# Retention decays carried by per-head rotary tables instead of decayed copies of queries and keys

## The chip, the cores and the metric

The kernel runs on one core of a Trainium2 chip. The metric is the device time of one execution in microseconds (us), as the median of three runs. Engine names are those of the profile: PE is TensorE (PEld its weight loads), DVE is VectorE, ACT is ScalarE, POOL is GpSimd, SP is the engine that issues most DMAs from one queue, in order.

## The reference

One step of a one-layer encoder on 1024 prompt frames and 8 streams of 16 new frames: 1152 tokens, nine tiles of 128 (tiles 0 to 7 are the prompt, tile 8 holds the streams). A projection feeds differential attention and retention, their outputs a second projection, and then a gated MLP with a convolution. The change concerns retention only:

```
qr = rotary(heads(qr), pos)
kr = rotary(heads(kr), pos) * R_K_DIM ** -0.5
def retention_chunk(state, q, k, v, log_gamma):          # per head, L tokens
    decay  = where(i >= j, gamma ** (i - j), 0)
    o      = ((q k^T) * decay) v + (q state) * gamma ** (i + 1)
    state  = gamma ** L * state + (k * gamma ** (L - 1 - j))^T v
```

with four heads and gamma of head h equal to 1 - 2^(-5-h).

## The kernel before

**Stages.** Start and first projections; attention over the prompt; attention of the streams against their caches (the "decode" stage, from about 462 us); retention (from about 560 to 645 us); output projection; MLP. In all of them PE takes projection work in small pieces ("dense units") between the pieces of the stage itself: `fill(ns)` puts in dense matmuls worth so many ns while any are left. The order of PE's instructions is that of the program; a scheduler orders those of the other engines and of SP's queue.

**Rotary.** `evac` takes a projected tile of 128 tokens and two heads out of PSUM. For `qr` and `kr` it multiplies by cosine and sine (three DVE operations, L242 to L245), adds on POOL (L246), and stores the result to the DRAM scratch `d_qr` or `d_kr`. The table of a tile comes by a load into `cs` (L238, two buffers), or, for the last `qr` unit, from `rope`, which is loaded whole in the decode stage (L810).

**Retention.** The loop goes over the tiles in the order 8, 0, 1, ..., 7. In step n, `rflip(t)` transposes the queries of tile t (L959, copied by ACT to `QT`) and its keys (L969, copied to `KT`), and makes decayed copies `Qd` (DVE, L965) and `Kd` (POOL, L975). `rout(t-1)` then does the previous tile: L994 is `AT` times values, L996 is `Qd` times state, L1000 is `Kd` times values for the state update. After it `load_t(t+1)` loads queries, keys and values of the tile after next (L952) into the tags `ldqr`, `ldkr`, `ldvr`, two buffers each: tile t+1 takes the buffers of tile t-1. Last in the step `rscore(t)` does L983, and DVE multiplies by the decay mask to make `AT` (L985).

So PE's order in one step is L959, L969 (tile t), L994/L996, L1000 (tile t-1), L983 (tile t), and then L959, L969 of tile t+1. The output of a tile is normalised and stored to `d_on` (L1041); `pro` reads it back (`on`, L910) and multiplies it by `sgr` (L912) on POOL for the next stage.

Of the kernel before, what the change touches and what calls it, by code (L numbers as in the profile page):

```python
# [32 lines left out]

C_ID, C_J, C_J16, C_SELD, C_SEL, C_HALF, C_SUM = 0, 128, 256, 384, 512, 768, 770
C_W = 802
R_DP, R_QP, R_KP, R_KE, R_KO, R_DS, R_QE, R_QO = 0, 512, 1024, 1028, 1032, 1036, 1548, 2060
R_P, R_W = 1036, 2572
TH, CW = NTOK // 2, NTOK // 4
ORD = (0, 4, 1, 5, 2, 6, 3, 7, 8)
GROUPS = (2, 2, 4, 3, 4, 3, 4)  # L40
# [8 lines left out]
def body(ctx: ExitStack, tc: tile.TileContext, i):  # L49
    nc = tc.nc  # L50
    V, S, G, T = nc.vector, nc.scalar, nc.gpsimd, nc.tensor
# [58 lines left out]
    aux = wst.enter_context(pool("stg", side="right"))  # L110
# [67 lines left out]
    units, pend, prog = [], [], {"cur": None, "bal": 0.0, "now": 0.0, "done": 0, "lim": 99, "rope": None}  # L178
# [51 lines left out]
    def evac(pfx, c, t, ps_, rope=None):  # L230
        d = dst_of(pfx, c)(t)
        sg = aux.tile([128, 256], F32, tag="sg", bufs=3, name="sg")
        if pfx in ("qr", "kr"):
            if rope is not None:
                cs = rope[:, t]
            else:
                cs = aux.tile([128, 2, 64], F32, tag="cs", bufs=2, name="cs")
                nc.sync.dma_start(cs, i["rope"][t * 128:(t + 1) * 128])  # L238
            tm = aux.tile([128, 2, 2, 64], F32, tag="rot", bufs=2, name="rot")
            pv = ps_.rearrange("p (h a d) -> p h a d", h=2, a=2)  # L240
            sb = cs[:, 1].unsqueeze(1).to_broadcast([128, 2, 64])
            V.tensor_tensor(out=sg.rearrange("p (a d) -> p a d", d=64), in0=ps_.rearrange("p (a d) -> p a d", d=64),  # L242
                            in1=cs[:, 0].unsqueeze(1).to_broadcast([128, 4, 64]), op=ALU.mult)
            V.scalar_tensor_tensor(out=tm[:, :, 0], in0=pv[:, :, 1], scalar=-1.0, in1=sb, op0=ALU.mult, op1=ALU.mult)
            V.tensor_tensor(out=tm[:, :, 1], in0=pv[:, :, 0], in1=sb, op=ALU.mult)  # L245
# [24 lines left out]
    with ExitStack() as st:  # L270
# [176 lines left out]
        for tok in "a0 w0 a1 w1 x5 a2 w2 a3 x6 x7 a4 x8 a5 a6 a7 w3".split():  # L447
            z_, n = tok[0], int(tok[1:])
# [48 lines left out]
        for n_, nm in enumerate(("lambda_q1", "lambda_k1", "lambda_q2", "lambda_k2")):  # L497
# [10 lines left out]
                               in1=ident_all[:, C_HALF:C_HALF + 1], op0=ALU.mult, op1=ALU.add)  # L508
# [26 lines left out]
    with ExitStack() as st:  # L535
# [158 lines left out]
        for n_ in range(8 * NH):  # L694
            h, qb = divmod(n_, 8)
# [18 lines left out]
    with ExitStack() as st:  # L714
        dp = st.enter_context(pool("dec"))
# [101 lines left out]
        for b in range(NB + 1):  # L817
            if b < NB:
# [3 lines left out]
                KT = dflip(b)  # L822
# [103 lines left out]
    with ExitStack() as st:  # L926
        rp = st.enter_context(pool("ret"))
# [9 lines left out]
        def c4(off):
            if off < R_P:
                return rc[:, off:off + 512].rearrange("p (h c) -> p h c", h=NH)
            c_ = rp.tile([128, NH, 128], F32, tag="Qd" if off == R_QO else "os", bufs=2, name="c4")  # L940
            nc.sync.dma_start(c_.rearrange("p h c -> p (h c)"), i["rpack"][:, off:off + 512])
            return c_
# [12 lines left out]
        def rflip(t):  # L955
            q, k, v = lds[t]
            pq = rt()
            for h in range(NH):
                T.transpose(pq[:, h], q[:, h], ident)  # L959
            QT = rp.tile([128, NH, 128], F32, tag="QT", bufs=2, name="QT")  # L960
            S.copy(QT, pq)
            qd = []
            for off in ((R_QP,) if t < 8 else (R_QE, R_QO)):
                x_ = rp.tile([128, NH, 128], F32, tag="KT" if qd else "Qd", bufs=2, name="Qd")
                V.tensor_tensor(out=x_, in0=pq, in1=c8[off] if t == 8 else c4(off), op=ALU.mult)  # L965
                qd.append(x_)
            pk = rt()
            for h in range(NH):
                T.transpose(pk[:, h], k[:, h], ident)  # L969
            KT = rp.tile([128, NH, 128], F32, tag="KT", bufs=2, name="KT")  # L970
            S.copy(KT, pk)
            kd = []
            for off in ((R_KP,) if t < 8 else (R_KE, R_KO)):
                x_ = rp.tile([128, NH, 128], F32, tag="QT" if kd else "Kd", bufs=2, name="Kd")
                G.tensor_tensor(out=x_, in0=k, in1=rc[:, off:off + 4].unsqueeze(2).to_broadcast([128, NH, 128]),  # L975
                                op=ALU.mult)
                kd.append(x_)
            return QT, KT, qd, kd
# [597 lines left out]
def _consts():  # L1576
# [3 lines left out]
    f = np.float32  # L1580
    n = np.arange(128)
# [22 lines left out]
    even = (n // 16) % 2 == 0  # L1604
    for h in range(NH):
        g = 1.0 - 2.0 ** (-5.0 - h)
        dec = np.where(ii >= jj, g ** np.maximum(ii - jj, 0), 0.0) * sc
        c = slice(h * 128, h * 128 + 128)
        rp[:, R_DP:][:, c] = dec
        rp[:, R_DS:][:, c] = np.where(ii // 16 == jj // 16, dec, 0.0)  # L1610
        rp[:, R_QP:][:, c] = g ** (n + 1.0)[None]
        rp[:, R_QE:][:, c] = (g ** (t16 + 1.0) * even)[None]
        rp[:, R_QO:][:, c] = (g ** (t16 + 1.0) * ~even)[None]
        rp[:, R_KP + h] = g ** (127.0 - n) * sc
        rp[:, R_KE + h] = g ** (15.0 - t16) * even * sc
        rp[:, R_KO + h] = g ** (15.0 - t16) * ~even * sc
# [38 lines left out]
```

## Time and profile before

| | |
|---|---|
| median of three runs | 1551.61 us (1546.86 to 1553.54) |
| the profiled execution | 1546.16 us, of which the span is 1544.3 us |
| PE busy | 1502.5 us, 97% of the span |
| DVE, ACT, POOL busy | 964.3, 601.4, 232.2 us |
| mean granted clock of PE | 0.990 |

The span runs from the first to the last instruction. An engine's busy share is a mean over all stages; PE's pieces overlap in the array, so a busy PE is not one at its peak. A row of the timeline gives start, duration, engine, line, operation, output and inputs, and in brackets the idle time ahead of it with what ended it.

### The profile page before, as it was taken

Reading aid. Unit: us, or ns where it says so; the run is one execution under the profiler, and the core shown is the slowest. Engines: PE = TensorE matmul, PEld = TensorE weight load, DVE = VectorE, ACT = ScalarE, POOL = GpSimd, SP = SyncE. Lnnn points to the kernel's source line nnn. Section 1 sums busy time; section 2 is a strip of 40 time slices with the busy share of each in tenths; the row PEclk is TensorE's granted clock in tenths of the full one; section 3 lists DMA queues with packets and bytes.
Section 4 is the critical chain, followed back from the end, with each engine's and each line's share of the span. In section 5 each row is a group of like instructions: output and inputs, shape, how many; then the busy total and the mean of one; then the engine's idle time right before and its main releaser. Section 6 shows DMA issues by size and latency. Waiting matters only on the chain.

```text
span 1544.3 us, 27022 instructions
## 1 busy us (share of the span) xinstructions
PE 1502.5 (97%) x10580; PEld 1369.4 (89%) x10580; DVE 964.3 (62%) x1735; ACT 601.4 (39%) x1167; POOL 232.2 (15%) x335
## 2 busy tenths in 40 slices
PE   6999999999999999999999999999999999999998
PEld 5867899999898898878899999999999988888786
DVE  4701237888765424553499877877788758254695
ACT  4501124555332433455564444444444455021212
POOL 1000021111121111343212111110111100000051
PEclk8999999999999999999999999999999999999999
DMA  9865331111319657675532222222222237132232
GB/s 295 270 253 181 121 107 49 54 46 50 110 61 338 217 200 222 224 249 191 171 119 86 82 73 74 72 71 80 77 75 71 80 119 270 35 116 88 95 134 109
DMA packets 191515, 205.98 MB, mean 133 GB/s; under 512 B 11357, under 2 KB 149899, under 8 KB 191388
## 3 DMA queue, kind: packets, MB, share of 16 engines
q1 hardware_dynamic: 172412, 189.31, 37.7%
q10 hardware_dynamic: 18976, 14.95, 3.0%
q8 instruction: 83, 1.36, 0.4%
q14 instruction: 44, 0.36, 0.1%
HBM read 154.66 MB, written 49.56 MB: 132 GB/s over the span
## 4 chain that ended last, share of the span: by engine, by line
PE 56%; DVE 2%; DMA 1%; issue 0%; ACT 0%; SPq 0%; POOL 0%; POOLq 0%; DVEq 0%; ACTq 0%
PE pb L1342 5%; PE pb L1344 5%; PE pb L1343 5%; PE dn L62 3%; PE dn L64 3%; PE dn L63 3%; PE pf L64 3%; PE pf L63 3%; PE pf L62 3%; PE dn L1342 2%; PE dn L1344 2%; PE dn L1343 2%; PE tp L1342 2%; PE tp L1344 2%; PE tp L1343 2%; PE tp L63 2%
## 5 line engine op out<-in xcount | busy, mean ns | idle before, releaser
L62 PE MATMUL dn<-w,hhi 128*128 128x256 f32 x648 | 189.7, 293 | 0.0
L64 PE MATMUL dn<-w,hlo 128*128 128x256 f32 x648 | 181.9, 281 | 0.0
L63 PE MATMUL dn<-w,hhi 128*128 128x256 f32 x648 | 181.6, 280 | 0.0
L62 PEld LDWEIGHTS dn<-w,hhi 128*128 128x128 f32 x648 | 122.5, 189 | 11.4 <-issue 10.2
L64 PEld LDWEIGHTS dn<-w,hlo 128*128 128x128 f32 x648 | 122.6, 189 | 7.5 <-issue 7.5
L63 PEld LDWEIGHTS dn<-w,hhi 128*128 128x128 f32 x648 | 122.7, 189 | 4.3 <-issue 4.2
L1288 DVE SCALAR_TENSOR_TENSOR y<-U,cv,y 128x1168 f32<-128x1168 f32 x88 | 124.2, 1429 | 3.0 <-ACT y L1285 2.1
L58 ACT CAST sl<-raw 128x512 fp32r<-128x512 f32 x65 | 40.3, 622 | 108.8 <-PE pb L1343 93.7
L58 ACT CAST se<-raw 128x512 fp32r<-128x512 f32 x66 | 41.1, 624 | 100.2 <-PE dn L1343 48.4
L62 PE MATMUL dn<-hhi,w 128*128 128x384 f32 x192 | 69.9, 364 | 0.0
L246 POOL TENSOR_TENSOR sg<-sg,rot 128x256 f32<-128x256 f32 x36 | 28.1, 780 | 272.2 <-DVE rot L245 229.5
L63 PE MATMUL dn<-hlo,w 128*128 128x384 f32 x192 | 65.0, 339 | 0.0
L64 PE MATMUL dn<-hhi,w 128*128 128x384 f32 x192 | 65.0, 339 | 0.0
L1294 POOL COPY tails<-U 128x18 f32<-128x18 f32 x44 | 23.7, 538 | 271.7 <-DVE U L1359 183.1
L59 DVE TENSOR_TENSOR w<-raw,w 128x512 fp32r<-128x512 f32 x56 | 39.0, 712 | 37.0 <-ACT w L58 24.7
L1285 ACT ACTIVATE y<-U,cv 128x1168 f32<-128x1168 f32 x44 | 60.2, 1367 | 4.5 <-DVE U L1363 0.5
L1514 DVE TENSOR_TENSOR facc<-facc,pf 128x512 f32<-128x512 f32 x54 | 36.8, 681 | 39.0 <-PE pf L64 39.0
L632 ACT ACTIVATE e<-sc,sm 128x128 f32<-128x128 f32 (+7 forms) x64 | 47.3, 744 | 30.9 <-DVE sm L631 30.1
L62 PE MATMUL dn<-woh,mh 128*128 128x512 f32 x144 | 57.9, 402 | 0.0
L58 ACT CAST w<-raw 128x512 fp32r<-128x512 f32 x56 | 33.3, 619 | 60.3 <-PE dn L63 33.8
L58 ACT CAST ew<-wr 128x512 fp32r<-128x512 f32 x24 | 14.6, 619 | 108.1 <-PE tp L63 84.2
L64 PE MATMUL dn<-woh,ml 128*128 128x512 f32 x144 | 56.5, 393 | 0.0
(427 smaller groups left out, 4861.8 us busy)
## 6 DMA issues: line engine op xcount, KB each, us to landing
wa<-in_w_ada SPq DMA_DIRECT2D x48, 512.0 KB, 8.6
raw<-in_w_up SPq DMA_DIRECT2D x88, 256.0 KB, 2.9
raw<-in_w_in SPq DMA_DIRECT2D x56, 256.0 KB, 4.2
wr<-in_w_down SPq DMA_DIRECT2D x48, 256.0 KB, 3.7
gr<-d_g SPq DMA_DIRECT2D x20, 576.0 KB, 3.7
d_g<-y SPq DMA_DIRECT2D x22, 512.0 KB, 2.6
kc<-in_cache_k SPq DMA_DIRECT2D x8, 1024.0 KB, 7.9
vc<-in_cache_v SPq DMA_DIRECT2D x8, 1024.0 KB
```

The costliest lines, as they stand in the source:

```text
L58: S.copy(hi, src)
L59: V.tensor_tensor(out=lo, in0=src, in1=hi.bitcast(F32), op=ALU.subtract)
L62: T.matmul(out, lhsT=sh, rhs=mh, start=first, stop=False)
L63: T.matmul(out, lhsT=sh, rhs=ml, start=False, stop=False)
L64: T.matmul(out, lhsT=sl, rhs=mh, start=False, stop=last)
L632: S.activation(out=e[:, hf, 0:nk], in_=s_[:, 0:nk], func=ACTF.Exp, bias=sm[:, hf:hf + 1], scale=1.0, accum_out=sm[:, 2 + hf:3 + hf])
L1285: S.activation(out=y[:, j0:j1], in_=U[:, j0:j1], func=ACTF.Identity, scale=wconv[0][:, kt:kt + 1], bias=bconv[:, kt:kt + 1])
L1288: V.scalar_tensor_tensor(out=y[:, j0:j1], in0=U[:, j0 + j:j1 + j], scalar=wconv[j][:, kt:kt + 1], in1=y[:, j0:j1], op0=ALU.mult, op1=ALU.add)
L1342: T.matmul(o, lhsT=sh, rhs=mh, start=st_, stop=False, skip_group_check=True)
L1343: T.matmul(o, lhsT=sh, rhs=ml, start=False, stop=False, skip_group_check=True)
L1344: T.matmul(o, lhsT=sl_, rhs=mh, start=False, stop=en, skip_group_check=True)
L1514: V.tensor_tensor(out=facc[t][:, sl], in0=facc[t][:, sl], in1=p_, op=ALU.add)
```

## The change

The rotary tables now exist for each head, and one set for queries and one for keys: for queries cosine and sine are multiplied by gamma^(age+1), for keys by gamma^(left) and the key scale, where age is a token's place in its tile (its stream for tile 8) and left the number of tokens behind it there. The rotated queries and keys are thus decayed already. The mask, once a decay matrix, becomes a constant of the head (gamma^-128, or gamma^-16 for tile 8) where i >= j. For the prompt's tiles `Qd` and `Kd` go: `rout` takes `QT` and the loaded keys themselves. For tile 8 the copies stay as selections of even and odd streams, the two `Kd` on ACT instead of POOL. Three of the constant tables that were loaded for tile 8 become one.

```diff
-                cs = aux.tile([128, 2, 64], F32, tag="cs", bufs=2, name="cs")
-                nc.sync.dma_start(cs, i["rope"][t * 128:(t + 1) * 128])
+                cs = aux.tile([128, 2, 2, 64], F32, tag="cs", bufs=2, name="cs")
+                nc.sync.dma_start(cs, i["rope"][int(pfx == "kr"), t * 128:(t + 1) * 128, c // 128:c // 128 + 2])
...
-        prog["rope"] = dp.tile([128, NT, 2, 64], F32, name="rope")
-        nc.sync.dma_start(prog["rope"], i["rope"].rearrange("(t p) a d -> p t a d", p=128))
+        prog["rope"] = dp.tile([128, NT, 2, 2, 64], F32, name="rope")
+        nc.sync.dma_start(prog["rope"].rearrange("p t h a d -> p t (h a d)"),
+                          i["rope"][0, :, 2:4].rearrange("(t p) h a d -> p t (h a d)", p=128))
...
             S.copy(QT, pq)
             qd = []
-            for off in ((R_QP,) if t < 8 else (R_QE, R_QO)):
-                x_ = rp.tile([128, NH, 128], F32, tag="KT" if qd else "Qd", bufs=2, name="Qd")
-                V.tensor_tensor(out=x_, in0=pq, in1=c8[off] if t == 8 else c4(off), op=ALU.mult)
-                qd.append(x_)
+            if t == 8:
+                for off in (R_QE, R_QO):
...
             S.copy(KT, pk)
             kd = []
-            for off in ((R_KP,) if t < 8 else (R_KE, R_KO)):
-                x_ = rp.tile([128, NH, 128], F32, tag="QT" if kd else "Kd", bufs=2, name="Kd")
-                G.tensor_tensor(out=x_, in0=k, in1=rc[:, off:off + 4].unsqueeze(2).to_broadcast([128, NH, 128]),
-                                op=ALU.mult)
-                kd.append(x_)
+            if t == 8:
+                for off in (R_KE, R_KO):
+                    x_ = rp.tile([128, NH, 128], F32, tag="Kd", bufs=2, name="Kd")
+                    S.activation(out=x_, in_=k, func=ACTF.Copy, scale=rc[:, off:off + 1])
+                    kd.append(x_)
+            else:
+                qd, kd = [QT], [k]
...
-        c8 = {off: c4(off) for off in (R_QO, R_QE, R_DS)}
+        ds = rp.tile([128, NH, 128], F32, tag="os", bufs=2, name="ds")
+        nc.sync.dma_start(ds.rearrange("p h c -> p (h c)"), i["rpack"][:, R_DS:R_DS + 512])
```

PE's order is the same in both kernels, but for the operands. In the middle of the retention loop PE has the following rows for the keys of tile 5 and the state update of tile 4; first before (`ld_7157` holds the keys of tile 5, `ld_7099` the values of tile 4, `Kd_7124` its decayed keys, which wait for POOL):

```order
L959 MATMUL rt_7168<-ident_all_72,ld_7155 128x128 [waits DMAHW2_49,DVE_49]
L969 MATMUL rt_7177<-ident_all_72,ld_7157 128x128 [waits DMAHW3_49,DVE_49]
L994 MATMUL rt_7186<-ld_7099,AT_7166 128x128 [waits DMAHW6_49,DVE_49]
L996 MATMUL rt_7186<-state_6323,Qd_7115 128x128
L1000 MATMUL rt_7195<-ld_7099,Kd_7124 128x128 [waits Activation_49,Pool_49]
L983 MATMUL rt_7237<-QT_7173,KT_7182 128x128 [waits DVE_49]
```

and then in the changed kernel (`ld_7133` holds the keys of tile 5, `ld_7079` and `ld_7077` the values and keys of tile 4):

```order
L953 MATMUL rt_7144<-ident_all_72,ld_7131 128x128 [waits DMAHW0_49,PE_49]
L965 MATMUL rt_7151<-ident_all_72,ld_7133 128x128 [waits DMAHW7_49,DVE_49]
L993 MATMUL rt_7158<-ld_7079,AT_7142 128x128 [waits DMAHW4_49,DVE_49]
L995 MATMUL rt_7158<-state_6323,QT_7093 128x128
L999 MATMUL rt_7167<-ld_7079,ld_7077 128x128 [waits Activation_49]
L981 MATMUL rt_7209<-QT_7149,KT_7156 128x128 [waits DVE_49,Activation_49]
```

The last reader of a tile's loaded keys was POOL's `Kd` behind L969; it is now L999, after the transposes of the next tile.

SP's queue shows what that does to the loads. Before, in the same part of the loop (keys `ld_7157` tile 5, `ld_7217` tile 6, `ld_7293` tile 7; values `ld_7005`, `ld_7099`, `ld_7159` tiles 3, 4 and 5; queries `ld_7155`, `ld_7215`, tiles 5 and 6; `os_6990`, `os_7084` outputs of tiles 1 and 2):

```order
L952 DMA ld_7005<-d_vr_61 128x512 [waits DMAHW1_49,PE_49]
L952 DMA ld_7155<-d_qr_59 128x512 [waits DMAHW2_49,PE_49]
L952 DMA ld_7157<-d_kr_60 128x512 [waits DMAHW3_49,PE_49,Pool_49]
L1041 DMA d_on_65<-os_6990 128x512 [waits DMAHW4_49,DVE_49,Activation_49]
L910 DMA on_7232<-d_on_65 128x512 [waits DMAHW5_49,DMAHW0_49]
L952 DMA ld_7099<-d_vr_61 128x512 [waits DMAHW6_49,PE_49]
L952 DMA ld_7215<-d_qr_59 128x512 [waits DMAHW7_49,PE_49]
L952 DMA ld_7217<-d_kr_60 128x512 [waits PE_49,Pool_49]
L1041 DMA d_on_65<-os_7084 128x512 [waits DMAHW1_49,DVE_49,Activation_49]
```

and in the changed kernel (keys `ld_6987` tile 3, `ld_7077` tile 4, `ld_7133` tile 5; values `ld_6989`, `ld_7079`, `ld_7135` of the same tiles; queries `ld_7131`, `ld_7187`, tiles 5 and 6; `os_6974`, `os_7064` outputs of tiles 1 and 2):

```order
L946 DMA ld_6987<-d_kr_60 128x512 [waits DMAHW5_49,PE_49]
L946 DMA ld_6989<-d_vr_61 128x512 [waits DMAHW6_49]
L911 DMA on_7204<-d_on_65 128x512 [waits DMAHW7_49,DMAHW4_49]
L946 DMA ld_7131<-d_qr_59 128x512 [waits DMAHW0_49,PE_49]
L1040 DMA d_on_65<-os_6974 128x512 [waits DMAHW1_49,DVE_49,Activation_49]
L913 DMA sgr_7294<-d_gr_62 128x512 [waits DMAHW2_49,Pool_49]
L946 DMA ld_7077<-d_kr_60 128x512 [waits DMAHW3_49,PE_49]
L946 DMA ld_7079<-d_vr_61 128x512
L946 DMA ld_7187<-d_qr_59 128x512 [waits DMAHW5_49,PE_49]
L1040 DMA d_on_65<-os_7064 128x512 [waits DMAHW6_49,DVE_49,Activation_49]
L946 DMA ld_7133<-d_kr_60 128x512 [waits DMAHW7_49,PE_49]
L946 DMA ld_7135<-d_vr_61 128x512
```

The keys of a tile stood one place behind its queries and two tiles ahead of its values; they now stand with its values, behind the output of the tile three before.

## Rows read from the trace of the kernel before

**Rows 1.** The page: the span, and busy time of each engine (us, share of the span, instructions).

```profile
span 1544.3 us, 27022 instructions
PE 1502.5 (97%) x10580; PEld 1369.4 (89%) x10580; DVE 964.3 (62%) x1735; ACT 601.4 (39%) x1167; POOL 232.2 (15%) x335
```

**Rows 2.** Busy time by stretches: the start of the retention stage, where dense units are left, and the loop of tiles 0 to 7, where none are. Columns: stretch, length, busy us (and instructions) of PE, PEld, DVE, ACT, POOL, granted clock of PE, DMA share, GB/s.

```profile
560.00:580.00 20.00, 19.74 (x171) 19.32 (x170) 5.29 (x9) 7.37 (x15) 3.08 (x3) 1.00 0.97 327
605.00:645.00 40.00, 36.20 (x311) 34.48 (x310) 25.43 (x72) 18.15 (x80) 15.84 (x15) 1.00 0.82 267
```

**Rows 3.** The timeline of PE in the retention loop: L969 of tile 2; then from L1000 of tile 4 to L994 of tile 5; then L969 of tile 7 and L1000 of tile 6.

```profile
611.62 0.60 PE L969 MATMUL rt<-ident_all,ld 128*128 128x128 f32 x4
...
629.65 1.06 PE L1000 MATMUL rt<-ld,Kd 128*128 128x128 f32 x8
630.54 1.06 PE L983 MATMUL rt<-QT,KT 128*128 128x128 f32 x8
631.44 0.60 PE L959 MATMUL rt<-ident_all,ld 128*128 128x128 f32 x4
631.87 0.60 PE L969 MATMUL rt<-ident_all,ld 128*128 128x128 f32 x4
632.55 0.49 PE L994 MATMUL rt<-ld,AT 128*128 128x128 f32 x2
...
637.10 0.60 PE L969 MATMUL rt<-ident_all,ld 128*128 128x128 f32 x4
637.54 0.39 PE L994 MATMUL rt<-ld,AT 128*128 128x128 f32 x2
...
639.32 1.06 PE L1000 MATMUL rt<-ld,Kd 128*128 128x128 f32 x8
```

**Rows 4.** The timeline of SP's queue in the same loop: the values of tile 2, the store of tile 0's output and its load back, the keys of tile 7, the values of tile 6.

```profile
611.76 0.38 SPq L952 DMA_DIRECT2D ld<-d_vr  x1
...
615.03 0.32 SPq L1041 DMA_DIRECT2D d_on<-os  x1
...
620.88 0.32 SPq L910 DMA_DIRECT2D on<-d_on  x1
...
627.74 0.32 SPq L952 DMA_DIRECT2D ld<-d_kr  x1
...
630.74 0.32 SPq L952 DMA_DIRECT2D ld<-d_vr  x1
```

**Rows 5.** DMA issues of the whole span: count, KB each, median us from issue to landing, where the trace has it.

```profile
raw<-in_w_up SPq DMA_DIRECT2D x88, 256.0 KB, 2.9
...
d_kr<-sg ACTq DMA_DIRECT2D x18, 128.0 KB, 1.7
...
ld<-d_qr SPq DMA_DIRECT2D x9, 256.0 KB, 5.2
ld<-d_kr SPq DMA_DIRECT2D x9, 256.0 KB, 4.5
...
on<-d_on SPq DMA_DIRECT2D x9, 256.0 KB, 3.8
...
rope<-in_rope SPq DMA_DIRECT2D x1, 576.0 KB
```

**Rows 6.** Groups of instructions in the loop (605 to 645 us): busy us, mean ns of one, idle time ahead and what ended it.

```profile
L994 PE MATMUL rt<-ld,AT 128*128 128x128 f32 x64 | 12.6, 286 | 3.8 <-DVE AT L985 3.5
...
L975 POOL TENSOR_TENSOR Kd<-ld,rc 128x512 f32<-128x512 f32 x6 | 6.2, 1039 | 17.3 <-PE rt L1000 10.6 <-issue 6.7
...
L965 DVE TENSOR_TENSOR Qd<-rt,rc 128x512 f32<-128x512 f32 x7 | 4.8, 686 | 0.9 <-ACT QT L961 0.9
```

**Rows 7.** Busy time by single microseconds at three places where PE stood idle for a short time (columns as in rows 2).

```profile
238.00:239.00 1.00, 0.80 (x7) 0.66 (x5) 0.38 (x2) 0.73 (x2) 0.00 (x0) 1.00 0.00 0
239.00:240.00 1.00, 0.00 (x0) 0.00 (x0) 1.00 (x4) 0.82 (x3) 0.00 (x0) 1.00 0.00 0
240.00:241.00 1.00, 0.52 (x3) 0.47 (x4) 0.97 (x3) 0.77 (x4) 0.00 (x0) 0.87 0.10 18
241.00:242.00 1.00, 1.00 (x5) 1.00 (x5) 0.97 (x5) 0.38 (x1) 0.00 (x0) 0.50 0.83 237
242.00:243.00 1.00, 1.00 (x4) 1.00 (x4) 0.94 (x4) 0.48 (x3) 0.00 (x0) 0.50 0.67 194
243.00:244.00 1.00, 1.00 (x5) 1.00 (x5) 0.75 (x2) 0.70 (x4) 0.00 (x0) 0.50 0.25 75
244.00:245.00 1.00, 1.00 (x7) 0.96 (x6) 0.52 (x3) 0.38 (x2) 0.00 (x0) 0.92 0.25 84
...
470.00:471.00 1.00, 0.06 (x1) 0.00 (x0) 0.31 (x1) 0.00 (x0) 0.00 (x0) 1.00 1.07 356
471.00:472.00 1.00, 0.50 (x5) 0.50 (x6) 0.00 (x0) 0.00 (x0) 0.00 (x0) 1.00 1.14 350
472.00:473.00 1.00, 1.00 (x11) 1.00 (x10) 0.69 (x1) 0.01 (x1) 0.00 (x0) 1.00 1.12 370
```

**Rows 8.** The timeline at the start of the decode stage: the load of the second stream's keys, and what waited for the table and for those keys.

```profile
470.11 0.99 SPq L728 DMA_DIRECT2D kc<-in_cache_k  x1
...
473.69 0.42 DVE L242 TENSOR_TENSOR sg<-dn,rope 128x256 f32<-128x256 f32 x1 [0.80 <-DMA rope<-in_rope]
...
479.89 0.63 PE L744 MATMUL tp<-ident_all,kc 128*128 128x128 f32 x4 [0.55 <-DMA kc<-in_cache_k]
```

**Rows 9.** Busy time by stretches there (columns as in rows 2).

```profile
468.00:480.00 12.00, 10.00 (x85) 8.53 (x85) 6.32 (x14) 3.62 (x7) 2.96 (x4) 1.00 1.07 370
```

**Rows 10.** Who waited for whom over the whole span: us in total, times, longest.

```profile
DVE sg L242 <- PE dn L64: 26.8, 19, 2.8
```

More of the change, by code (lines that the diff above doesn't have):

```diff
@@ L35 @@
 C_W = 802
-R_DP, R_QP, R_KP, R_KE, R_KO, R_DS, R_QE, R_QO = 0, 512, 1024, 1028, 1032, 1036, 1548, 2060
-R_P, R_W = 1036, 2572
+R_DP, R_QE, R_QO, R_KE, R_KO, R_DS = 0, 512, 640, 768, 769, 776
+R_P, R_W = 776, 1288
 TH, CW = NTOK // 2, NTOK // 4
@@ L236, in evac @@
             else:
-                cs = aux.tile([128, 2, 64], F32, tag="cs", bufs=2, name="cs")
-                nc.sync.dma_start(cs, i["rope"][t * 128:(t + 1) * 128])
+                cs = aux.tile([128, 2, 2, 64], F32, tag="cs", bufs=2, name="cs")
+                nc.sync.dma_start(cs, i["rope"][int(pfx == "kr"), t * 128:(t + 1) * 128, c // 128:c // 128 + 2])
             tm = aux.tile([128, 2, 2, 64], F32, tag="rot", bufs=2, name="rot")
             pv = ps_.rearrange("p (h a d) -> p h a d", h=2, a=2)
[L241 to L245, printed above, removed]
+            V.tensor_tensor(out=sg.rearrange("p (h a d) -> p h a d", h=2, a=2), in0=pv,
+                            in1=cs[:, :, 0].unsqueeze(2).to_broadcast([128, 2, 2, 64]), op=ALU.mult)
+            V.scalar_tensor_tensor(out=tm[:, :, 0], in0=pv[:, :, 1], scalar=-1.0, in1=cs[:, :, 1],
+                                   op0=ALU.mult, op1=ALU.mult)
+            V.tensor_tensor(out=tm[:, :, 1], in0=pv[:, :, 0], in1=cs[:, :, 1], op=ALU.mult)
             G.tensor_tensor(out=sg, in0=sg, in1=tm.rearrange("p h a d -> p (h a d)"), op=ALU.add)
@@ L935, in body @@
         stt = rp.tile([128, NH, 128], F32, name="state")
[L937 to L942, printed above, removed]
         add_dense("gr", GR, 256, with_extra(rp))
@@ L962, in rflip @@
             qd = []
-            for off in ((R_QP,) if t < 8 else (R_QE, R_QO)):
-                x_ = rp.tile([128, NH, 128], F32, tag="KT" if qd else "Qd", bufs=2, name="Qd")
-                V.tensor_tensor(out=x_, in0=pq, in1=c8[off] if t == 8 else c4(off), op=ALU.mult)
-                qd.append(x_)
+            if t == 8:
+                for off in (R_QE, R_QO):
+                    x_ = rp.tile([128, NH, 128], F32, tag="Qd", bufs=2, name="Qd")
+                    V.tensor_tensor(out=x_, in0=pq, in1=rc[:, off:off + 128].unsqueeze(1).to_broadcast([128, NH, 128]),
+                                    op=ALU.mult)
+                    qd.append(x_)
             pk = rt()
@@ L984, in rscore @@
             AT = rp.tile([128, NH, 128], F32, tag="AT", bufs=1, name="AT")
-            V.tensor_tensor(out=AT, in0=pS, in1=c4(R_DP) if t < 8 else c8[R_DS], op=ALU.mult)
+            V.tensor_tensor(out=AT, in0=pS, in1=rc[:, R_DP:R_DP + 512].rearrange("p (h c) -> p h c", h=NH) if t < 8 else ds,
+                            op=ALU.mult)
             return AT
@@ L1604, in _consts @@
     even = (n // 16) % 2 == 0
+    gs = 1.0 - 2.0 ** (-5.0 - np.arange(NH))
     for h in range(NH):
-        g = 1.0 - 2.0 ** (-5.0 - h)
-        dec = np.where(ii >= jj, g ** np.maximum(ii - jj, 0), 0.0) * sc
         c = slice(h * 128, h * 128 + 128)
[L1609 to L1616, printed above, removed]
+        rp[:, R_DP:][:, c] = np.where(ii >= jj, gs[h] ** -128.0, 0.0)
+        rp[:, R_DS:][:, c] = np.where((ii >= jj) & (ii // 16 == jj // 16), gs[h] ** -16.0, 0.0)
+    rp[:, R_QE:R_QE + 128] = even[None]
+    rp[:, R_QO:R_QO + 128] = ~even[None]
+    rp[:, R_KE] = even
+    rp[:, R_KO] = ~even
     half = 64
@@ L1622, in _consts @@
     co, si = np.cos(ang), np.sin(ang)
-    rope = np.stack([co, si], 1).astype(f)
+    age = np.concatenate([np.arange(SEQ) % 128, np.tile(np.arange(TD), NB)])[:, None]
+    left = np.concatenate([127 - np.arange(SEQ) % 128, TD - 1 - np.tile(np.arange(TD), NB)])[:, None]
+    cs = np.stack([co, si], 1)[:, None]
+    rope = np.stack([cs * (gs ** (age + 1.0))[:, :, None, None],
+                     cs * (gs ** left.astype(float) * sc)[:, :, None, None]]).astype(f)
     rel = np.arange(384) - 255
```

## The prediction

> **What bounds the kernel now.** The page comes first: PE is busy for 97% of the span [rows 1], so an edit on another engine pays only where PE waits for that engine. Next, busy time by stretches, for the stage the change touches. While dense units are left (560 to 580 us) PE is busy for 19.74 of 20 us; in the loop over tiles 0 to 7 it is busy for 36.2 of 40 [rows 2]. The groups of that loop say who ends its waits: L994 lost 3.8 us, nearly all to the mask multiplication `AT`; L996 and L1000, the readers of `Qd` and `Kd`, are not named as waiting [rows 6]. The reader should see that the copies which go away were on nobody's path: POOL made a `Kd` in 1039 ns while itself idle, DVE a `Qd` in 686 ns. Last the timelines of PE and of SP's queue, for the question that the order raises: when may the next keys be loaded, and when are they needed?
>
> **The change, part by part.**
>
> *Removed work.* Eight `Qd` (8 x 0.69 = 5.5 us of DVE) and ten `Kd` (10.4 us of POOL) are worth nothing: they lie beside PE's matmuls, and the multiplication PE does wait for, `AT`, keeps its length and is followed by `Qd`, not preceded by it. The two smaller constant loads of tile 8 and its two `Kd` on ACT fall between 560 and 580 us, where dense matmuls cover all; without them a `Kd` would cost at most POOL's 1.04 us each.
>
> *The keys' buffer.* This is the term that counts. Keys have two buffers, so tile t+1 takes those of tile t-1. Before, these were free after the transposes and `Kd` of t-1, and the load ran a whole step ahead: the keys of tile 7 were issued at 627.74 and read by L969 at 637.10, 9.4 us later [rows 3, 4]. Now L1000 of tile t-1 reads them, and PE's order puts L969 of tile t+1 just behind it. In the rows: L1000 of tile 4 starts at 629.65 and ends at 630.71; L969 of the next flip starts at 631.87, only 1.16 us later [rows 3]. Into these 1.16 us a load of 256 KB must now fit. That SP can answer at once is seen in the values, which have always waited for the same L1000: issued at 630.74, 0.03 us after its end [rows 4].
>
> How long a load takes: `on`, of the same size and shape and issued in this loop, lands 3.8 us after issue; the keys' own median is 4.5, the queries' 5.2; the quickest 256 KB of the kernel, `raw` of the MLP, takes 2.9 [rows 5]. I take 3.8 for the loads of tiles 3 to 7 and keep 2.9 and 4.5 as bounds. A step is then L969 to the end of L1000, plus 0.03, plus 3.8. The first part, with `AT` long ready, is 637.10 to 639.32 + 1.06 = 3.28 us (the one flip that had no wait ahead of L994 [rows 3]). So a step lasts 7.11 us, and five of them, from L969 of tile 2 to that of tile 7, 35.55 us. Before it was 637.10 - 611.62 = 25.48. That adds 10.1 us. Loads for tiles 2 to 7 wait in this way, six in all; those of tiles 0 and 1 are issued while the dense units run.
>
> The first, tile 2, stands in SP's queue behind the streams' states and, by the order, about where the values of tile 2 stood: 611.76 [rows 4]. The DMAs are crowded there, so I take the keys' 4.5: it lands at 616.3 instead of being read at 611.62, +4.6 us. Together **14.7 us**; with 2.9 throughout 8.6 (+3.0 and 5 x 0.9 less), with 4.5 throughout 18.2.
>
> Queued behind the waiting load in SP are the values of the same tile, read a step later, the queries of the tile after, and `d_on`; none is needed within the step.
>
> *The clock.* Each step now has PE idle from the end of L959 (1.33 us after L1000's end, 631.44 + 0.60 against 630.71) until 3.83, so 2.5 us, six times. After an idle stretch of 1.68 us (0.20 + 1.00 + 0.48) the granted clock fell from 2.4 to 1.2 GHz: 0.87, 0.50, 0.50, 0.50, 0.92 in successive microseconds; after one of 1.44 us at 470 us it stayed at 1.00 [rows 7]. The fall is (0.13 + 1.5 + 0.08)/0.5 = 3.4 us at half speed, 1.7 us of work lost. The work from L969 to L959 is 4.6 us long, so most of a fall would lie in it. It need not happen at every gap, and a part can lie in the idle time: I take four falls of six, **6.8 us**, between 0 and 10.2.
>
> [...]
>
> *The rotary tables.* `rope` doubles from 576 KB [rows 5], and it is issued ahead of the second stream's keys, for which PE already waited 0.55 us [rows 8]. The DMAs move 370 GB/s there [rows 9], so 0.59 MB more costs **1.6 us** of PE's wait, at least 0 if the keys were late for another reason. DVE waits longer for the table (0.80 us now), which two PSUM buffers absorb. The 27 loads of `cs` go from 64 to 128 KB; in 19 waits at L242 it was PE that came last, not the table [rows 10], so they stay hidden; uncovered they would cost 64 KB / 370 GB/s = 0.2 us each.
>
> *Sum.* 14.7 + 6.8 + 1.6 = 23.1 us on 1546.16, the profiled run's own time: 1569.3. The median of the three runs lies 5.4 us above that execution, and the new time will be a median too: 1551.6 + 23.1, rounded to **1574**. A difference within 0.5% (8 us) cannot be told from no change here.
>
> **The rivals.**
>
> *The clock holds* (0.2): the wait as above, no fall: +16.3, 1568. For it: the gap at 470 us. Against it: the new gaps are longer than one that fell.
>
> *The load is quick* (0.12): out of a queue that is emptier than today's, keys land in 2.9 us: 8.6 + 1.6, and with gaps of 1.6 us, between those that did and did not drop the clock, nought to two falls: +10 to +14, 1562 to 1566; if `rope` too is hidden, 1560. Against it: all loads of 256 KB timed in this stage took longer.
>
> The page "DMA: Bandwidth & Descriptors" of the Trainium skill, section "Anatomy of one DMA — SWDGE (gpsimd) path", gives 2.0 us plus bytes at 436 GB/s, so as an estimate 2.6 us for 256 KB (for another issuing path). The buffer term would be 6.8 us and the time about 1560. The rows of this stage, 3.8 to 5.2, do not agree.
>
> *SP's queue holds the keys back* (0.09): the keys of tile 4 stand behind `sgr`, which waits for POOL, which waits for `on`, which waits for `d_on` of tile 0. That store took until 620.88 from 615.03 [rows 4]. If this chain ends after L1000 of tile 2, one more load of 3.8 us plus POOL's work is paid, about 5 us, and crowded loads at 4.5 add 3.5: 1583.
>
> *Not slower* (0.03): if the load landed within the 1.16 us between L1000 and L969, nothing would wait, and what stays is a shorter DVE queue ahead of `AT`, at best the 3.8 us of L994: 1548. It decides at 1.16 us; the shortest landing of the list, for half the bytes, is 1.7 [rows 5].
>
> **How the numbers follow.** The forecast holds 0.56, from 1570 to 1581 with its own bounds. The range reaches from the quick load with little else (1560) to the queue's delay with a run of the upper kind (1585), and leaves out the last rival and tails of the others. Faster 0.02; same 0.06, the rest of "not slower" and the quickest loads; slower 0.92.
>
> **What would show it.** In the changed kernel's own line numbers, L965 (the keys' transposes, L969 before) should have idle time ended by the DMA from `d_kr`, six times, 2 to 5 us each, and the steps of the loop should be 7 to 9 us apart, not 4.8. The clock of the stretch from 612 to 660 us should show 0.5 in single microseconds. L744 should wait about 2 us for the second stream's keys. The wait of L993 (L994 before) for `AT` should be gone. The forecast is wrong if L965 waits less than 1 us per tile, or if the time goes to another stage.

## The result and the profile after

The changed kernel takes 1561.39 us (median of 6 runs, 1557.68 to 1565.90); the kernel before, on the same chip, 1549.05 us (6 runs, 1544.10 to 1553.54). The ratio is 1.0089, 95% interval 1.0071 to 1.0107, so 11 to 17 us slower; the two medians alone lie 12.3 us (0.8%) apart. The profiled execution took 1557.68 us against 1546.16: 11.5 us more. The forecast was 1574, 22 us above the 1551.6 that it started from.

The page of the changed kernel, span and busy time (beside [rows 1]):

```profile
span 1555.9 us, 26986 instructions
PE 1500.9 (96%) x10580; PEld 1367.7 (88%) x10580; DVE 956.5 (61%) x1727; ACT 603.3 (39%) x1169; POOL 219.8 (14%) x325
```

PE has as many matmuls as before, and no more busy time. POOL lost 12 us and VectorE 8, and the span grew by 11.6: the time went into PE's waits. The loop's stretch of [rows 2], after the change:

```profile
605.00:645.00 40.00, 26.27 (x215) 25.23 (x216) 11.46 (x36) 12.01 (x54) 6.31 (x6) 0.91 0.66 207
```

The loop of the prompt's tiles is where it changed: PE is busy for 26.3 of these 40 us, against 36.2 in [rows 2], and the DMAs move 207 GB/s instead of 267. PE's timeline there, the transposes of keys of tiles 1 to 7 (L965, which answers to L969 in [rows 3]); in brackets the idle time ahead and what the profile says ended it:

```profile
602.95 0.66 PE L965 MATMUL rt<-ident_all,ld 128*128 128x128 f32 x4
...
614.73 1.08 PE L965 MATMUL rt<-ident_all,ld 128*128 128x128 f32 x4 [6.21 <-DMA ld<-d_kr]
...
622.31 0.63 PE L965 MATMUL rt<-ident_all,ld 128*128 128x128 f32 x4 [1.54 <-DVE os L1039]
629.48 0.63 PE L965 MATMUL rt<-ident_all,ld 128*128 128x128 f32 x4 [2.53 <-DMA ld<-d_kr]
635.76 0.63 PE L965 MATMUL rt<-ident_all,ld 128*128 128x128 f32 x4 [1.64 <-DVE os L1039]
642.07 0.63 PE L965 MATMUL rt<-ident_all,ld 128*128 128x128 f32 x4 [1.67 <-DVE os L1039]
648.21 0.63 PE L965 MATMUL rt<-ident_all,ld 128*128 128x128 f32 x4 [1.07 <-DMA ld<-d_kr]
```

Six of the seven have an idle gap ahead, 14.7 us in all. Before, the same seven instructions ran from 606.22 to 637.10:

```profile
606.22 0.66 PE L969 MATMUL rt<-ident_all,ld 128*128 128x128 f32 x4
```

so from tile 1 to tile 7 the time grew from 30.88 us to 45.26: +14.4. SP's queue gives the loads they wait for, those of the keys of tiles 2 to 7:

```profile
608.69 0.38 SPq L946 DMA_DIRECT2D ld<-d_kr  x1
619.47 0.32 SPq L946 DMA_DIRECT2D ld<-d_kr  x1
626.40 0.38 SPq L946 DMA_DIRECT2D ld<-d_kr  x1
632.82 0.32 SPq L946 DMA_DIRECT2D ld<-d_kr  x1
639.10 0.32 SPq L946 DMA_DIRECT2D ld<-d_kr  x1
645.40 0.32 SPq L946 DMA_DIRECT2D ld<-d_kr  x1
```

Read against PE's rows, the first load is read 6.0 us after its issue, the others after 2.84, 3.08, 2.94, 2.97 and 2.81. Three of the gaps are put down to VectorE's `os`, whose wait ended last by the records, but their loads are as old at that moment as in the others. Whether `os` would have held PE without the load is for an experiment.

The granted clock around the first gap, in stretches of 5 us (columns as in [rows 2]):

```profile
610.00:615.00 5.00, 0.28 (x2) 0.31 (x3) 0.00 (x0) 0.00 (x0) 0.00 (x0) 0.58 1.03 302
615.00:620.00 5.00, 5.00 (x35) 5.00 (x34) 0.53 (x3) 1.73 (x9) 0.00 (x0) 0.73 0.38 146
```

The clock fell from 2.4 to 1.2 GHz once, in the gap of 6.21 us, and a little over half of that fall lay where PE had nothing to do. In the five gaps of 1.1 to 2.5 us it stayed at 2.4: the clock is 1.00 in every microsecond from 618 to 652 us. At the decode stage PE waits longer for the second stream's keys, 2.33 us against the 0.55 of [rows 8]:

```profile
479.35 0.63 PE L744 MATMUL tp<-ident_all,kc 128*128 128x128 f32 x4 [2.33 <-DMA kc<-in_cache_k]
```

### The profile page after: what moved, and what is told of

Its sections match the earlier page's. It is cut to its first block, busy times and chain, and to the rows that moved or that the text cites. A ratio compares the mean times of both kernels' runs of the same rounds, so it can differ in the third digit from the quotient of the medians.

```text
span 1555.9 us, 26986 instructions
## 1 busy us (share of the span) xinstructions
PE 1500.9 (96%) x10580; PEld 1367.7 (88%) x10580; DVE 956.5 (61%) x1727; ACT 603.3 (39%) x1169; POOL 219.8 (14%) x325
## 4 chain that ended last, share of the span: by engine, by line
PE 83%; DMA 6%; DVE 5%; issue 2%; ACT 2%; SPq 2%; POOL 1%; POOLq 0%; ACTq 0%; DVEq 0%
PE dn L62 9%; PE dn L64 9%; PE dn L63 9%; PE pb L1342 5%; PE pb L1344 5%; PE pb L1343 5%; PE pf L64 3%; PE pf L62 3%; PE pf L63 3%; PE dn L1342 2%; PE dn L1344 2%; PE dn L1343 2%; PE tp L1342 2%; PE tp L1344 2%; PE tp L1343 2%
```

## The experiments

Theory A is that of the prediction: without a decayed copy the raw keys are held until L999 of their tile, so the next load into that buffer is issued with nothing left to hide it. The rivals are another pacer of the loop (the queries read from `QT`, VectorE's `os`, the queue of SP), and for the clock a fall at every gap. Ratios are to the kernel before on the same chip.

**e1_keys4: four buffers for the keys, in the same room.** Only tile 8 uses `Kd` now, so its two buffers are free for later keys.

```diff
-                ld[n_] = rp.tile([128, NH, 128], F32, tag="ld" + n_, bufs=2, name="ld")
+                ld[n_] = rp.tile([128, NH, 128], F32, tag="Kd" if n_ == "kr" and t in (2, 3, 6, 7) else "ld" + n_, bufs=2, name="ld")
```

> The changed kernel with one edit: the raw keys of tiles 2, 3, 6 and 7 go into the two Kd buffers, which only tile 8 uses, so that the keys rotate over four buffers in the same room, and no load of keys waits for the tile just computed. Theory A (the loss is the wait for the buffer of the raw keys): the loads of keys are issued a tile earlier, PE's waits for DMA before the transposes of keys fall from about 15 us in sum to under 2, the fall of the clock at 611 to 618 is gone, and the loop is as short as before the change, so that 14 to 15 us come back: the changed kernel's profiled 1557.7 less 14.8 is 1543, below the kernel before (1544 to 1553). Rival B (something else paces the loop now: the queue of stores and loads on SP, or VectorE's os and AT that come late): the waits move to other instructions, each tile still takes 6 us or more, and the time stays at 1555 to 1562.

Measured: 1545.09 us, ratio 0.9997 (0.9983 to 1.0011). The loop's stretch, the first and last of its transposes of keys, the issue of the last keys, and PE's largest wait from 600 to 650 us (in total, times, longest):

```profile
605.00:645.00 40.00, 36.37 (x305) 34.93 (x306) 19.29 (x59) 19.57 (x82) 10.87 (x10) 1.00 0.79 259
```

```profile
603.83 0.66 PE L965 MATMUL rt<-ident_all,ld 128*128 128x128 f32 x4
...
634.76 0.60 PE L965 MATMUL rt<-ident_all,ld 128*128 128x128 f32 x4
```

```profile
624.62 0.42 SPq L946 DMA_DIRECT2D ld<-d_kr  x1
```

```profile
PE rt L993 <- DVE AT L983: 3.6, 3, 1.5
```

The keys of tile 7 are issued 10.1 us before they are read, L965 is in no wait, and tiles 1 to 7 take 30.93 us, as before the change (30.88). The wait put down to `os` is gone too, though nothing was done about `os`: those gaps were the load's. All that the change cost comes back, and rival B falls. e9_keys4_again below repeats it.

**e2_copyk: POOL copies the keys again, without a decay.**

```diff
-                qd, kd = [QT], [k]
+                x_ = rp.tile([128, NH, 128], F32, tag="Kd", bufs=2, name="Kd")
+                G.tensor_copy(x_, k)
+                qd, kd = [QT], [x_]
```

> The changed kernel with POOL copying the raw keys of tiles 0 to 7 into Kd (no decay, only a copy), and L999's counterpart reading the copy: the buffer of the raw keys comes free after the transposes and the copy, as before the change, with no buffer more. Theory A (the wait for the buffer): the time falls as with four buffers of keys, to 1543 to 1548, and the loads of keys are issued 7 to 8 us ahead of the matmuls that read Kd. Rival B (another pacer in the loop): 1555 to 1562. If POOL's copy is slow enough to be late itself, L999 waits for POOL.

Measured: 1545.13 us, ratio 0.9996 (0.9983 to 1.0009). POOL's copy of the last keys, of tile 7:

```profile
635.58 0.61 POOL L976 COPY Kd<-ld 128x512 f32<-128x512 f32 x1 [2.66 <-PE rt L1001]
```

A copy that computes nothing restores the time. What POOL's multiplication did for the kernel before, on an engine that was idle, was to give the loaded buffer back early. One point of the expectation was not tested: POOL's copy was never late, so no wait of the matmuls for POOL is seen.

**e4_b_keys: of the change, only the raw keys, in the kernel before.** The decay of the keys is left out of the computation.

```diff
-            for off in ((R_KP,) if t < 8 else (R_KE, R_KO)):
+            for off in (() if t < 8 else (R_KE, R_KO)):
...
-            return QT, KT, qd, kd
+            return QT, KT, qd, kd or [k]
```

> The kernel before with one part of the change alone: the matmuls of the state's update read the raw keys for tiles 0 to 7 and the decayed copy of the keys is left out (so the decay of the keys is left out of the computation); the decayed queries, the tables and the masks stay. Theory A (the wait for the buffer of keys): the loop gets 13 to 17 us longer, as in the changed kernel, the waits before the transposes of keys end on DMA, and the time is 1560 to 1566. Rival B (the loss comes with the queries read straight from QT, the tables or the masks): 1546 to 1552 as before. In both, the state loads ahead of the loop keep their wait of 2 us and their fall of the clock if these come from the constants or the order that this kernel keeps.

Measured: 1561.39 us, ratio 1.0098 (1.0074 to 1.0121). PE's transposes of keys of tiles 1, 2, 4 and 7:

```profile
605.95 0.66 PE L969 MATMUL rt<-ident_all,ld 128*128 128x128 f32 x4
```

```profile
617.21 1.08 PE L969 MATMUL rt<-ident_all,ld 128*128 128x128 f32 x4 [5.70 <-DMA ld<-d_kr]
...
632.65 0.99 PE L969 MATMUL rt<-ident_all,ld 128*128 128x128 f32 x4 [2.07 <-DVE os L1040]
...
653.10 0.63 PE L969 MATMUL rt<-ident_all,ld 128*128 128x128 f32 x4 [1.40 <-DMA ld<-d_kr]
```

This edit alone makes the loss: from tile 1 to tile 7 47.15 us, +16.3, and a time like that of the whole change. Here the clock fell twice, at the gap of 5.70 us and behind the gap of 2.07 us: 0.50 in the two microseconds that follow it.

```profile
633.00:635.00 2.00, 2.00 (x12) 2.00 (x11) 0.00 (x0) 0.58 (x1) 0.00 (x0) 0.50 0.63 234
```

**e6_b_queries: of the change, only the queries.** The decay of the queries is left out of the computation.

```diff
-            for off in ((R_QP,) if t < 8 else (R_QE, R_QO)):
+            for off in (() if t < 8 else (R_QE, R_QO)):
...
-            return QT, KT, qd, kd
+            return QT, KT, qd or [QT], kd
```

> The kernel before with the other half of the change alone: for tiles 0 to 7 the matmuls read QT, and the decayed copy of the queries on VectorE (L965) is left out (so the decay of the queries is left out of the computation). Theory A (only the buffer of the raw keys costs): the time is that of the kernel before, 1544 to 1552, the loop from L969 of tile 2 to that of tile 7 stays at 25 to 26 us, and VectorE's 8 times 0.69 us are saved beside PE. Rival B (the queries read from QT hold its buffers a tile longer and bring a wait at L961 or L959): 2 us or more a tile, 1558 and above.

Measured: 1547.60 us, ratio 1.0014 (0.9998 to 1.0031). PE's largest wait in the loop is still that for `AT`, the next is of 0.3 us:

```profile
PE rt L994 <- DVE AT L985: 4.1, 4, 1.5
```

Tiles 1 to 7 take 603.89 to 635.32, 31.43 us (+0.55). Removing `Qd` shows no gain, as was said, and no wait at the transposes; the interval leaves room for a cost of up to 0.3%, far from the 2 us a tile of rival B.

**e5_keys_twice: the wait doubled.** The changed kernel, each load of keys of tiles 2 to 7 done twice.

```diff
+                if n_ == "kr" and t in range(2, 8):
+                    nc.sync.dma_start(ld[n_].rearrange("p h d -> p (h d)"), d_r[n_][rows])
```

> The changed kernel with the raw keys of tiles 2 to 7 loaded twice into the same buffer, the second load behind the landing of the first, so that PE waits for two landings instead of one. The later loads landed 2.8 to 3.1 us after their issue in the changed kernel, with gaps of PE of 1.1 to 2.5 us. Theory A (the landing of one load is the whole step, and the clock holds in short gaps): each of the six steps grows by 2.9 us, 17 us in sum, to 1575 on the profiled 1557.7. Theory C (the clock falls at each gap of this length, now 4 to 5.5 us, as it fell at the one gap of 6.2 us and not at the gaps up to 2.5): falls at four or more of the six gaps, each at 1 to 2 us for the matmuls that run at half clock, so 1581 to 1590. If neither, and the loads land on shared engines that were idle, the steps grow by less than 2 us: under 1570.

Measured: 1591.34 us, ratio 1.0282 (1.0249 to 1.0315), 30 us above the changed kernel. The transposes of keys of tile 1 and of tiles 2 to 7, with the six gaps, and the granted clock beside the second:

```profile
605.41 0.66 PE L967 MATMUL rt<-ident_all,ld 128*128 128x128 f32 x4
...
621.04 1.08 PE L967 MATMUL rt<-ident_all,ld 128*128 128x128 f32 x4 [10.07 <-DMA ld<-d_kr]
632.18 1.09 PE L967 MATMUL rt<-ident_all,ld 128*128 128x128 f32 x4 [5.10 <-DMA ld<-d_kr]
644.51 1.09 PE L967 MATMUL rt<-ident_all,ld 128*128 128x128 f32 x4 [5.09 <-DMA ld<-d_kr]
655.89 1.09 PE L967 MATMUL rt<-ident_all,ld 128*128 128x128 f32 x4 [5.14 <-DMA ld<-d_kr]
667.68 0.63 PE L967 MATMUL rt<-ident_all,ld 128*128 128x128 f32 x4 [4.46 <-DMA ld<-d_kr]
678.62 1.09 PE L967 MATMUL rt<-ident_all,ld 128*128 128x128 f32 x4 [4.24 <-DMA ld<-d_kr]
```

```profile
630.00:635.00 5.00, 2.82 (x14) 2.85 (x15) 0.00 (x0) 0.59 (x1) 0.00 (x0) 0.58 0.22 68
```

The gaps grew from 14.7 to 34.1 us, 19.4 in sum, near A's 17. From tile 1 to tile 7 it is 73.21 us (605.41 to 678.62), 28.0 more than in the changed kernel, so 8.5 of these are work at the lower clock; the fall behind the last gap comes on top. Theory C, the fall in at least four of the six gaps, holds, and the time lies 1 us above its 1581 to 1590: five of the six transposes run at half speed (1.08 or 1.09 us where 0.60 to 0.66 is usual), and a stretch at or just behind every gap shows a clock below 1. Where gaps are of 4 us and more, the clock term of the prediction is real; at the gaps that the change made it is nearly absent.

**e7_b_rope2: the load of the tables doubled in the kernel before.** The second half of what is loaded is read by nobody.

```diff
-        prog["rope"] = dp.tile([128, NT, 2, 64], F32, name="rope")
-        nc.sync.dma_start(prog["rope"], i["rope"].rearrange("(t p) a d -> p t a d", p=128))
+        rope2 = dp.tile([128, NT, 2, 2, 64], F32, name="rope")
+        nc.sync.dma_start(rope2.rearrange("p t h a d -> p t (h a d)"),
+                          i["rope2"].rearrange("(t p) h a d -> p t (h a d)", p=128))
+        prog["rope"] = rope2[:, :, 0]
```

> The kernel before with the load of the tables of rotation of the last stage doubled in bytes (the second half read by nobody), nothing else changed. Theory A (the doubled load takes 1.4 to 1.6 us more of engines that are full there, and the second cached keys are behind it): PE's wait for the second cached keys grows by 1.4 us, and the time by 1 to 2 us, unless a fall of the clock just ahead of it swallows the wait. Rival: the load lies beside others and nothing is moved: within 0.5 us of before.

Measured: 1546.34 us, ratio 1.0003 (0.9991 to 1.0015). The waits for the first and the second stream's keys, and the clock between them:

```profile
470.12 0.66 PE L744 MATMUL tp<-ident_all,kc 128*128 128x128 f32 x4 [1.60 <-DMA kc<-in_cache_k]
...
479.86 0.63 PE L744 MATMUL tp<-ident_all,kc 128*128 128x128 f32 x4 [0.71 <-DMA kc<-in_cache_k]
```

```profile
472.00:476.00 4.00, 4.00 (x27) 3.55 (x30) 2.01 (x6) 1.39 (x3) 0.74 (x1) 0.66 1.09 376
```

Inconclusive on the size: the second wait grew by 0.16 us only, but the clock fell between the two waits, which it did not in [rows 7], and PE was ready for the second 9.0 us after the first had ended, not 7.8 as before. What the table costs over many executions is 0.5 us, with bounds from -1.4 to 2.3.

It settles something else. The prediction was made on an execution in which the clock fell at 598 to 604 us; in the trace of this kernel, whose streams' states and constants are those of before, it does not:

```profile
598.00:600.00 2.00, 0.61 (x13) 0.49 (x16) 0.00 (x0) 0.00 (x0) 0.00 (x0) 0.79 0.14 42
600.00:602.00 2.00, 2.00 (x34) 1.53 (x30) 0.00 (x0) 0.57 (x5) 0.00 (x0) 0.50 0.00 0
```

```profile
598.00:600.00 2.00, 2.00 (x41) 1.82 (x40) 0.17 (x1) 1.14 (x8) 0.41 (x1) 1.00 0.04 8
600.00:602.00 2.00, 1.73 (x16) 1.56 (x15) 1.37 (x5) 0.38 (x1) 0.60 (x1) 1.00 0.00 0
```

The first fence is the kernel before, the second e7_b_rope2. In the profiled execution of the changed kernel the wait for those states is shorter and the fall absent as well. PE is 0.5 us ahead of the kernel before at the second stream's keys (479.35 against 479.89) and 3.3 at the keys of tile 1 (602.95 against 606.22); since a kernel without the change shows the same states' wait and no fall, these 2.7 us are no gain of the change.

**e3_keys4_rope and e8_rope_late: the table loaded in two parts**, on e1_keys4. In e3_keys4_rope tiles 0 and 1 come first and the rest behind the second stream's keys; in e8_rope_late the cut is at tile 4 and the rest stands behind the first cached values. The edit of e8_rope_late, without that of the four buffers:

```diff
-        nc.sync.dma_start(prog["rope"].rearrange("p t h a d -> p t (h a d)"),
-                          i["rope"][0, :, 2:4].rearrange("(t p) h a d -> p t (h a d)", p=128))
...
+        rope_part(0, 4)
...
                 load_vc(b)
+                if b == 0:
+                    rope_part(4, NT)
```

> The four buffers of keys as in e1_keys4, and the load of the tables of rotation split: tiles 0 and 1 ahead, the rest behind the second cached keys in SP's queue. Theory A (1.4 us of the change's loss are the wait for the second cached keys behind the doubled tables): PE's wait for kc there falls by about 1.4 us, and the time lies 1 to 2 us under e1_keys4. Rival: those keys come no earlier, since all DMA engines are full there, or the wait goes to the next load: same time as e1_keys4 within 0.5 us.

Measured for e3_keys4_rope: 1548.27 us, ratio 1.0012 (1.0000 to 1.0024): 3 us more than e1_keys4 where 1 to 2 less were expected. PE's two largest waits from 466 to 492 us, and ACT's rows at the longest of it:

```profile
PE tp L744 <- ACT KT L746: 3.6, 1, 3.6
PE tp L744 <- DMA kc<-in_cache_k: 1.4, 1, 1.4
```

```profile
484.88 0.33 ACTq L253 DMA_DIRECT2D d_qr<-sg  x1
485.31 0.70 ACT L763 ACTIVATE e<-sc,sm 128x528 f32<-128x528 f32 x1 [8.85 <-DMA vc<-in_cache_v]
```

The second stream's keys are not waited for, but neither are they in e1_keys4, where the table is whole. There PE waits longer for the first stream's keys, the clock falls behind that wait, and the second come in time:

```profile
470.91 0.85 PE L744 MATMUL tp<-ident_all,kc 128*128 128x128 f32 x4 [2.45 <-DMA kc<-in_cache_k]
```

So these two runs do not show that the split saved a wait. What is new in e3_keys4_rope is that ACT stands still for 8.85 us, until the cached values `vc` have landed, which neither instruction reads. The order of the instructions suggests why. First the load of `vc` on SP, then the store and what stands behind it on ACT:

```
L733 DMA vc<-in_cache_v 128x4x512 [waits DMAHW0_49]
```

```
L253 DMA d_qr<-sg 128x256 [waits DMAHW0_49,Pool_49]
L763 ACTIVATE e,sm<-sc,sm 128x528 [waits DVE_49,PE_49]
L746 COPY KT<-tp 128x512 [waits PE_49] x2
```

Each DMA's issue waits for one of eight completion semaphores, DMAHW0 to DMAHW7, which the program takes in turn over all queues. The load of `vc` and, eight DMAs on, the store have the same, so the store has to wait until `vc` has landed; in e1_keys4, with one load fewer in front of `vc`, the pair is another.

> The four buffers of keys of e1_keys4, and the tables of rotation split otherwise than in e3_keys4_rope: tiles 0 to 3 ahead, tiles 4 to 8 behind the first cached values instead of ahead of them. In e3_keys4_rope a store of rotated queries on ACT's queue came 6 us late (issued at 484.88, its data done at 478.78), its predecessor on the same completion semaphore being the load of the first cached values, and PE then waited 3.6 us for ACT. Theory A (that wait for the semaphore's earlier user is what the split cost): with the second part issued behind those values the store's predecessor is another small store, ACT's idle time of 8.85 us there is gone, PE does not wait for ACT, and the time lies 2 to 4 us under e3_keys4_rope, at 1543 to 1546. Rival B (the split itself delays the tables, VectorE and so PE): PE waits for VectorE or ACT there as in e3_keys4_rope, 1547 to 1550.

> The kernel of e1_keys4 again, beside e8_rope_late on the same chip: 1543 to 1547, within 0.15% of the kernel before, and no wait of L965 for the loads of keys. If e8_rope_late gains anything over it by the split, 1 to 2 us.

Measured together: e8_rope_late 1543.96 us, ratio 0.9986 (0.9974 to 0.9998); e9_keys4_again 1545.57 us, ratio 0.9998 (0.9987 to 1.0009). In e8_rope_late PE waits in that stretch only for the first stream's keys, and ACT no longer for `vc`:

```profile
PE tp L744 <- DMA kc<-in_cache_k: 2.2, 1, 2.2
```

That is what was expected if the store was held by the semaphore's former user; the place of the cut moved as well. e8_rope_late is the fastest kernel of the study, 0.14% below the kernel before: its interval only just leaves out no change. It overlaps that of the four buffers alone, which are level with before, so a gain by the split itself (1.6 us between the medians) is not shown.

## Why the prediction was right, and where its sizes were off

The mechanism is shown from both sides: undone by e1_keys4 and e2_copyk, made alone by e4_b_keys. The sum, 23.1 us, was 1.4 to 2.1 times the 11 to 17 us measured. That 1561.39 lies inside the stated range, 1.4 us above its lower end, is owed to the rival of the quick load, which set that end, and not to the sum. Term by term:

- **The keys' buffer, forecast 14.7, measured 13.0.** From tile 1 to tile 7 the stretch grew by 14.4, of which 1.4 belong to the clock (below). Two errors partly cancelled. The first load was forecast at +4.6 with a landing of 4.5 us; it took 6.0 us among DMAs that moved 302 GB/s, and cost 6.4. The five others were forecast with 3.8 and took 2.8 to 3.1, so five steps cost 8.0 less the clock's 1.4, 6.6 instead of 10.1. The step's form was exact: L965 at 629.48 to the next issue at 632.82 is 3.34 us (forecast 3.28 + 0.03), and the load follows. What failed is the reason for 3.8: it was the landing of loads in the loop before, where the DMAs moved 267 GB/s and the keys stood 0.5 us behind the queries in SP's queue. The five loads now met DMAs that stood almost idle: 0 to 39 GB/s in the microsecond in which each was issued, here for tile 3, against 236 for the load at 627.74 of [rows 4]; first after, then before:

```profile
619.00:620.00 1.00, 1.00 (x11) 1.00 (x11) 0.53 (x3) 0.72 (x6) 0.00 (x0) 1.00 0.00 0
```

```profile
627.00:628.00 1.00, 0.92 (x9) 0.68 (x8) 0.76 (x3) 0.67 (x2) 0.90 (x2) 1.00 0.78 236
```

The page of e4_b_keys, which stalls in the same way, has a median landing of 2.9 us for the loads of keys where [rows 5] have 4.5. "Against it: all loads of 256 KB timed in this stage took longer" took the old traffic for the new. That the quiet is the cause is argued: no run changed the traffic alone.

- **The Trainium skill's time for a load.** By the fit on the page "DMA: Bandwidth & Descriptors", section "Anatomy of one DMA — SWDGE (gpsimd) path", 2.0 us plus bytes at 436 GB/s, the estimate for 256 KB is 2.6 us, for another issuing path. The five loads were read 2.8 to 3.1 us after issue, nearer to it than to the 3.8 taken, and the first, in crowded DMAs, 6.0.
- **The clock, forecast 6.8, measured 1.4.** One fall of six gaps, not four. Its price: L965 of tile 2 to the next issue of keys is 619.47 - 614.73 = 4.74 us where the later step has 3.34. The forecast's gap of 2.5 us followed from a landing of 3.8; with 2.9 four of the later gaps are of 1.1 to 1.7 us, which the rival of the quick load had at "nought to two falls". That gaps of this size may or may not bring a fall, as [rows 7] had it, stands: 2.53 us here did not, 2.07 us in e4_b_keys did.
- **The Trainium skill's case of a loop that waits.** The page "TensorE: Matmul & The Clock Gate", section "HAM oscillation — how this bites in real kernels", describes a loop whose matmuls for a tile take less time than its wait for the DMA, and has a fall at every tile of it. In the changed kernel a step's matmuls take 4.6 us (629.48 to the end of L953 at 634.12). The first wait, 6.21 us, is longer, and there the clock fell; the others, 1.1 to 2.5, are shorter, and it held. In e5_keys_twice, where waits of 4.2 to 10.1 us come up to these 4.6 us or exceed them, it fell at all six. So far the traces agree; the fall behind 2.07 us in e4_b_keys does not.
- **The table, forecast 1.6.** In the profiled execution the second stream's keys were waited for 1.78 us longer, but the first stream's 0.71 shorter (0.74 against 1.45). Alone, in e7_b_rope2, the doubled load costs 0.5 us and not provably anything. The wait is there; a part of it only takes the place of a fall of the clock or of the wait ahead.
- **The base, not forecast.** Against the execution that the sum was made on, the changed kernel's was 3.3 us ahead when the loop began, the wait for the table already paid: two falls of the clock, at 400 and at 600 us, happened to that execution of before. The second is absent from e7_b_rope2 too; the first is there in e1_keys4, which has the change, though not in the changed kernel's execution, with 1.00 (first the kernel before, then e1_keys4):

```profile
400.00:405.00 5.00, 4.65 (x25) 4.68 (x26) 3.78 (x11) 1.30 (x2) 0.72 (x1) 0.66 0.42 144
```

```profile
400.00:405.00 5.00, 5.00 (x31) 5.00 (x31) 3.44 (x8) 1.36 (x4) 0.73 (x1) 0.70 0.49 156
```

They make the difference of the two profiled executions smaller than the loop's 14.4; over all runs the loss is 11 to 17 us. The median that the forecast was added to, 1551.61, came out at 1549.05 over six runs, 2.6 us lower.

- **Edits at nothing.** The removed `Qd` (e6_b_queries) and `Kd` (e2_copyk against e1_keys4, 1545.13 against 1545.09) show no gain, as said. The wait for `AT` was to be gone; 2.3 us of it are left of the 3.5 before.

Of the rivals, the quick load (0.12) described the five later loads (5.6 us for them, 6.6 measured) and the one fall, but not the first load (3.0, against 6.4). That its +10 to +14 us hold the 12.3 between the medians is in part luck. SP's queue held the keys back once by the chain that its rival names, and for less than it said. The keys of tile 4 stand behind `sgr`, which waits for POOL's reading of the buffer:

```profile
624.69 1.27 POOL L914 TENSOR_TENSOR on<-on,sgr 128x512 f32<-128x512 f32 x1 [3.17 <-DMA d_on<-os]
```

```profile
625.98 0.32 SPq L913 DMA_DIRECT2D sgr<-d_gr  x1
```

`sgr` is issued 0.02 us after POOL's end (625.96), and the keys at 626.40, 0.78 us after L999 of tile 2 had ended (624.56 + 1.06): 0.8 us of the gap of 2.53, not 5 us. The first load of keys is 1.5 us behind its L999 (606.12 + 1.06 to 608.69), behind other issues in SP's queue; the other four are within 0.03 us. The forecast's "2 to 5 us each" for L965's gaps holds for one of six (2.53); one is longer and four are shorter. The steps of 6.1 to 7.6 us lie below its 7 to 9 for three of five.

## What to carry to other kernels

A copy on an idle engine may be worth its time for what it releases: before it is removed, ask who reads the source last afterwards, and whether the next load into that buffer still has a step to hide in. If the copies' own buffers become free, give them to the loads; that undid the whole loss at no cost in memory. When pricing a load that a stalled loop will wait for, look at what the DMAs will carry at the moment of its issue, not at the landings of the loop that does not stall: here 2.8 to 3.1 us stood against the 3.8 taken over.

## What was not expected of the hardware

A gap's length alone does not decide a fall of the clock in this range: PE's gap of 2.07 us in e4_b_keys was followed by one and the gap of 2.53 us in the changed kernel was not, while all gaps above 4 us in these runs have a stretch below 1 beside them. Nor does one kernel decide it: the gap of 1.68 us at 239 us in [rows 7] was followed by a fall, and in e7_b_rope2, which does the same up to there, a gap of 1.67 us at the same place left the clock at 1.00 from 240 to 245 us.

A DMA's issue can wait for a DMA it has nothing to do with: one more load in SP's queue gave a store on ACT's queue the load of `vc` as the former user of its completion semaphore, ACT stood still for 8.85 us, and PE waited 3.6 us for ACT's next copy. With the load cut elsewhere and issued behind `vc`, as in e8_rope_late, that was gone.
